# Other cuts for the feed-forward groups and the first output projection in a two-layer diffusion trunk on one core

## The chip, the cores and the metric

One Trainium2 chip, one of its NeuronCores. The metric is the device time of one execution in microseconds. Before the change the median of 3 runs is 2937.39 us (2935.81 to 2938.43).

Five engines work on the core, each through its own instructions in order: TensorE (PE in the profile; PEld is its weight loading), VectorE (DVE), ScalarE (ACT), GpSimd (POOL) and SyncE (SP), which here only issues DMAs.

## The reference, cut to what matters

Input are 512 latent tokens and 128 context tokens, 640 in all, of width 1024. They pass two layers and a last norm. Each layer is: feed-forward, token mixing, feed-forward. Every one of these three parts does

```
h = rmsnorm(x, norm_g) * (1 + m_scale) + m_shift        # m: from the conditioning vector
x = x + [0.5 *] m_gate * part(h)
part of a feed-forward: (silu(h @ w_gate) * (h @ w_up)) @ w2       # inner width 2816
part of a mixing:       concat(y_a, y_b) @ w_out                   # 1024 x 1024
m = silu(cond) @ mod_w[i] + mod_b[i]                               # 9 vectors of 1024 for each layer
```

The mixing of layer 0 is retention beside a gated recurrent block, that of layer 1 a state-space layer beside a delta-rule recurrence. After the norm at the end `y_prompt` and `y_sample` are written, along with four context states.

## The kernel before, in words

**Layout and arithmetic.** Activations lie transposed: `x[d]` is a tile of 128 features by 640 tokens, with 8 such tiles; tokens are worked in two halves of 320 (`h` = 0, 1). Every large product is made three times over from parts (`mm3`, L426): activation and weight are each split into a rounded part and a rest (`whi`/`wlo` for weights, `hs`/`ls` for the normed input, the pairs in `hl` for inner activations), and three matmuls of 128 x 128 by 320 columns sum into one PSUM bank. A weight piece of 128 x 512 is loaded (`load_piece`, L370), rounded by ScalarE (L380) and its rest formed by VectorE (L381), or by GpSimd where `eng=PL` is given (the first two weight tiles of a stage; L400 does the same for the very first). There are 5 buffers for raw pieces and 8 each for `whi` and `wlo`.

**Stages.** Seven, in this order: `f01` (layer 0, feed-forward 1), `m0`, `f02`, `f11`, `m1`, `f12`, `fin`. 

**A feed-forward stage** (`ffn`, L575). The inner width of 2816 is cut into 22 tiles of 128. They are worked in groups, 7, 7, 6 and 2 tiles (`GROUPS`, `GL`, L28). For one group, first the tiles go "up": gate and up product, silu, multiplication, split into a pair of `hl`; 96 matmuls per tile in the plain form. In `f02` from tile 12 on and in `f12` from tile 5 on a form with 7 block products (`up7`) takes their place; it needs sums of the normed input that are made once (`quarters`, L513, started three tiles earlier, in a pool that takes space from the setup of layer 1's state-space part). Then the group goes "down" through `w2`: for each of the four column blocks `dp`, 4 banks of 3 x (tiles of the group) matmuls sum into PSUM banks of the pool `psa` (two banks, tag `acc`), and `add_res` (L545) on VectorE adds each bank, times the gate, to `x`.

**The last group** of a stage goes down in `last_pass` (L551) instead: all of the first half of the tokens, then all of the second. Behind each bank's update the squares for the next norm are summed (`sq`, L452). When the first half is through, its sum over features is taken by a matmul with ones (`stat(0)`, L464), and then `apply(0)` (L476) makes the next stage's normed input for the first half, while the second half of the last pass still goes on; `stat(1)` comes after the last bank, and `apply(1)` after the next stage's first two weight tiles have used the first half. The last group's weights are 4 pieces now, of the 8 buffers.

**Output projections.** `m0` ends in `out_proj` (L749): 8 input tiles, 6 of which go down as above (`w_out0a`, 18 matmuls a bank) and 2 through `last_pass` (`out_last`, L743, with `w_out0b`). At its start `x` is loaded back from DRAM (`load_x`), since the mixing needs its slots. `m1` has its own code for the first 6 (`first_out`) and shares `out_last`.

**Modulation vectors.** Those not needed at once are made by VectorE along the way, in `f01` (9 vectors) and `f11` (7). One vector is 9 steps (`mod_steps`, L329): in each of 8 steps a 512 KB block of `mod_w` is loaded and two 128 x 1024 multiply-adds go into a pair of accumulators (`ma`, L335 and L337, one buffer each), and a ninth step has TensorE reduce them (L342) and finish (L349 to L354). The accumulators come free for the next vector when the L342 matmuls of this one are done. `extra()` (L951) runs 3 steps in `f01` and 2 in `f11`; it is called after each up tile and at the start of each `dp` of a group that goes down (not of the last group), and its first two calls in the program do nothing. What is left is done in one go by `finish_mods()` (L944, called at L679) after the up tiles of the last but one group, ahead of that group's way down.

**Order of the work.** The order on each engine is set beforehand by a planner that runs the program against its own costs: of the instructions that could start, it takes the one that stands first in the program. So an engine may run ahead into later parts when it has nothing else, but what stands earlier in the program goes first as soon as it can start. In `f02` VectorE also prepares the state-space part (`s5_prep`, one call per up tile).

Of the kernel before, what the change touches and what calls it, by code (L numbers as in the profile page):

```python
# [18 lines left out]
P = 128  # L19
D = 1024  # L20
KT = D // P
# [3 lines left out]
HALF = T // 2  # L25
DFF = 2816
NF = DFF // P
GROUPS = [7, 7, 6]  # L28
GL = 2

SEVEN = {(0, 2): 12, (1, 2): 5}
RAWS = 5
# [23 lines left out]
def pack(x):  # L56
    f = np.ascontiguousarray
# [21 lines left out]
    out["w_in0"] = f(w.reshape(KT, P, 12, 256).transpose(2, 1, 0, 3)).reshape(12, P, KT * 256)  # L79
    out["w_v0"] = f(w[:, :, 2].reshape(2, 4, P, 512).transpose(0, 2, 1, 3)).reshape(2, P, 2048)  # L80

    def out_w(n, w, order):
        w = w.reshape(KT, P, 4, 256)[order]
        out[n + "a"] = f(w[:6].transpose(2, 1, 0, 3)).reshape(4, P, 6 * 256)
        out[n + "b"] = f(w[6:].transpose(1, 2, 0, 3)).reshape(P, 2048)
    out_w("w_out0", x["l0_w_out"], [4, 5, 6, 7, 0, 1, 2, 3])
    gates = np.stack([x["l0_lru_wa"], x["l0_lru_wx"]]).reshape(2, 2, 4, 2, 64, 64)
    bd = np.zeros((2, 2, 4, P, P), np.float32)
    bd[..., :64, :64] = gates[:, :, :, 0]
# [4 lines left out]
    out["c1"] = _consts1()  # L94
    w = x["l1_w_in"].reshape(KT, P, 10, 256)
    out["w_in1"] = f(w.transpose(2, 1, 0, 3)).reshape(10, P, KT * 256)
    out_w("w_out1", x["l1_w_out"], list(range(8)))

    def lora_in(a):
        return np.moveaxis(a, 0, 1).reshape(4, P, P) if a.ndim == 3 else a.reshape(4, P, P)  # L100
# [112 lines left out]
def _build(nc, tc, I, O, ctx):  # L213
# [192 lines left out]
    def part(w):  # L406
        return lambda k, o: w(k * 256 + o)
# [141 lines left out]
                                     x[d][:, c0 + a:c0 + b], ALU.mult, ALU.add)  # L549

    def last_pass(w, hl, g, nxt):  # L551
        for h in range(2):
            c = hs_(h)
            for d in range(KT):
                ps = bank(psa, HALF, "acc") if d % 2 else bank(psp, HALF, "gu")
                for i in range(2):
                    mm3(ps, *w(2 * (d // 2) + i, d % 2 * P), hl[i][0][:, c], hl[i][1][:, c], i == 0, i == 1)
                add_res(d, h, ps, g)
                if nxt is not None:
                    nxt.sq(d, h)  # L560
                    if h == 0 and d == 6:
                        ACT.activation(warm, x[d][:, :1], AF.Abs_reciprocal_sqrt, scale=0.0, bias=epsn)
                        DVE.tensor_scalar_mul(zero, warm, 0.0)
                        warmed.append(1)
                    if h == 1 and d == 1:
                        nxt.stat(0)
                        nxt.apply(0)
        if nxt is not None:
            if nxt.final:
                for k in range(4):  # L570
                    nxt.finish(k)
            nxt.stat(1)


    def ffn(l, which, n, gt, mk_next):  # L575
# [52 lines left out]
        for G in GROUPS + [GL]:  # L628
# [52 lines left out]
            if f0 + G == NF:  # L681
                if quarters:
                    close_pool("xt")
                src = I[f"w2_{which}"][l, :, :, f0 * 256:].rearrange("d p n -> p d n")
                ws = [split_piece(load_piece(src[:, d:d + 1, :])) for d in range(4)]
                nxt = nxt()
                last_pass(lambda k, o: [t[:, k % 2 * 256 + o:k % 2 * 256 + o + P] for t in ws[k // 2]], hl, gt(), nxt)
                return nxt
# [52 lines left out]
        return out  # L741

    def out_last(hl, name, g, nxt, w=None):  # L743
        w = w or part(weight(I[name + "b"]))
        nxt = nxt()
        last_pass(w, hl, g, nxt)
        return nxt

    def out_proj(src, name, g, mk_next):  # L749
        nxt = mk_next(load=True)  # L750
        hl = [split_slot(t) for t in src]
        load_x(xs)
        for dp in range(4):
            w = weight(I[name + "a"][dp], 1536)
            for e in range(2):
                for h in range(2):
                    c = hs_(h)
                    ps = bank(psa, HALF, "acc")
                    for i in range(6):
                        mm3(ps, *w(i * 256 + e * P), hl[i][0][:, c], hl[i][1][:, c], i == 0, i == 5)  # L760
                    add_res(2 * dp + e, h, ps, g)
        return out_last(hl[6:], name, g, nxt)

    def log_sigmoid(dst, src, n):
        st = slot()
# [1281 lines left out]
```

## Time and profile before

| what | value |
|---|---|
| median of 3 runs | 2937.39 us |
| the profiled execution | 2936.11 us, its span 2934.3 us |
| PE busy | 2778.1 us, 95% of the span, 25440 matmuls |
| PEld busy | 2627.8 us, 90% |
| DVE busy | 2013.1 us, 69% |
| ACT busy | 1128.8 us, 38% |
| POOL busy | 258.4 us, 9% |
| mean granted TensorE clock | 0.978 of full |

The span is what the profiler saw between the first and the last instruction; 1.8 us of the execution lie outside. A share of busy time is a mean over stages: in most of a feed-forward stage PE is busy without a break, and what it loses lies in a few places, above all where one stage passes to the next. In the rows further down, a bracket behind a row is the idle time of its engine just before it and what ended it; "x" and a number is a count of instructions, merged where they follow each other.

### The profile page before, as it was taken

The page shows a single profiled execution, that of the slowest core. Times are in us where ns is not written, and L with a number is a line of the kernel's source. Part 1 is how long each engine was busy: PE and PEld are TensorE (multiplying, and loading weights), DVE is VectorE, ACT ScalarE, POOL GpSimd, SP SyncE. Part 2 cuts the span into 40 slices and gives each one's busy share as a digit, 9 for nine tenths or more (in the row PEclk, how much of TensorE's full clock was granted, in tenths as well). Part 3 has the DMA queues.
Part 4 walks back from the last instruction along what each step waited for, and adds up shares of the span by engine and source line. Part 5 has one row for each costly group of instructions (what it writes and reads, how often), then busy time and mean ns, then how long its engine had stood idle before and what let it go on. Part 6 is the DMA issues. An engine that isn't in the chain of part 4 may idle for free.

```text
span 2934.3 us, 62170 instructions
## 1 busy us (share of the span) xinstructions
PE 2778.1 (95%) x25440; PEld 2627.8 (90%) x25440; DVE 2013.1 (69%) x4347; ACT 1128.8 (38%) x2337; POOL 258.4 (9%) x226
## 2 busy tenths in 40 slices
PE   6999999999999999998999999998889988999997
PEld 4999999877789998998999999987677877999997
DVE  7686773864798977868665664676766536758676
ACT  4222223584443223435222223334555434424233
POOL 2000000130010000002000001221222103000001
PEclk8999999999999999999999999999999999999999
DMA  8464643211213442234444544352000021123231
GB/s 287 145 198 136 183 142 130 94 44 62 97 60 118 127 116 80 80 97 144 145 142 129 152 139 138 105 156 88 4 4 4 9 87 67 59 79 93 74 91 58
DMA packets 164446, 305.41 MB, mean 104 GB/s; under 512 B 25664, under 2 KB 47808, under 8 KB 164032
## 3 DMA queue, kind: packets, MB, share of 16 engines
q1 hardware_dynamic: 164160, 301.44, 32.8%
q8 instruction: 199, 3.26, 0.5%
q14 instruction: 87, 0.71, 0.1%
HBM read 276.95 MB, written 24.42 MB: 103 GB/s over the span
## 4 chain that ended last, share of the span: by engine, by line
PE 58%; DVE 11%; issue 5%; ACT 2%; POOL 1%; DMA 1%; POOLq 0%; DVEq 0%; ACTq 0%; SPq 0%
PE gu L428 11%; PE gu L429 11%; PE gu L427 11%; PE acc L427 5%; PE acc L428 5%; PE acc L429 5%; PE m L1626 2%; PE acc L1626 1%; PE gu L1626 1%; PE gu L1290 1%; DVE ma L337 1%; DVE s L548 1%; DVE t L496 1%; DVE wlo L381 1%; PE m L429 1%
## 5 line engine op out<-in xcount | busy, mean ns | idle before, releaser
L427 PE MATMUL gu<-s,whi 128*128 128x320 f32 x2804 | 876.1, 313 | 0.8 <-ACT s L1376 0.8
L429 PE MATMUL gu<-s,wlo 128*128 128x320 f32 x2804 | 870.9, 311 | 1.4 <-DVE wlo L381 1.4
L428 PE MATMUL gu<-s,whi 128*128 128x320 f32 x2804 | 871.0, 311 | 0.3 <-DVE s L415 0.3
L380 ACT CAST whi<-raw 128x512 fp32r<-128x512 f32 x624 | 375.9, 610 | 773.0 <-PE acc L428 384.1
L427 PEld LDWEIGHTS gu<-s,whi 128*128 128x128 f32 x2804 | 528.6, 189 | 9.0 <-ACT whi L380 3.5
L429 PEld LDWEIGHTS gu<-s,wlo 128*128 128x128 f32 x2804 | 528.4, 188 | 3.6 <-DVE wlo L381 1.6
L428 PEld LDWEIGHTS gu<-s,whi 128*128 128x128 f32 x2804 | 528.6, 189 | 2.6 <-DVE s L415 0.6
L381 DVE TENSOR_TENSOR wlo<-raw,whi 128x512 fp32r<-128x512 f32 x576 | 381.2, 673 | 152.5 <-ACT whi L380 148.9
L427 PE MATMUL acc<-s,whi 128*128 128x320 f32 x1456 | 452.2, 311 | 6.2 <-DVE s L548 6.2
L429 PE MATMUL acc<-s,wlo 128*128 128x320 f32 x1456 | 451.7, 310 | 0.7 <-DVE wlo L381 0.7
L428 PE MATMUL acc<-s,whi 128*128 128x320 f32 x1456 | 451.6, 310 | 0.0
L427 PEld LDWEIGHTS acc<-s,whi 128*128 128x128 f32 x1456 | 274.1, 188 | 10.6 <-DVE s L548 6.3
L337 DVE SCALAR_TENSOR_TENSOR ma<-mw,cT,ma 128x1024 f32<-128x1024 f32 x224 | 277.0, 1277 | 0.0
L429 PEld LDWEIGHTS acc<-s,wlo 128*128 128x128 f32 x1456 | 274.2, 188 | 1.2 <-DVE wlo L381 0.9
L428 PEld LDWEIGHTS acc<-s,whi 128*128 128x128 f32 x1456 | 274.1, 188 | 0.2 <-issue 0.2
L548 DVE SCALAR_TENSOR_TENSOR s<-acc,hg,s 128x320 f32<-128x320 f32 (+1 forms) x336 | 137.2, 434 | 154.7 <-PE acc L429 152.3
L414 ACT CAST s<-t 128x320 fp32r<-128x320 f32 x212 | 97.0, 458 | 250.7 <-DVE t L641 214.4
L641 DVE TENSOR_TENSOR t<-t,gu 128x320 f32<-128x320 f32 x122 | 59.1, 485 | 167.2 <-PE gu L429 163.5
L400 POOL TENSOR_TENSOR s<-s,s 128x512 fp32r<-128x512 f32 x28 | 40.3, 1464 | 1031.5 <-PE gu L428 891.9
L415 DVE TENSOR_TENSOR s<-t,s 128x320 fp32r<-128x320 f32 x212 | 108.3, 511 | 22.5 <-ACT s L414 22.4
L381 POOL TENSOR_TENSOR wlo<-raw,whi 128x512 fp32r<-128x512 f32 x48 | 67.5, 1425 | 568.8 <-ACT whi L380 555.7
L427 PE MATMUL gu<-s,s 128*128 128x320 f32 x304 | 92.7, 338 | 22.3 <-ACT s L501 20.7
(464 smaller groups left out, 4511.2 us busy)
## 6 DMA issues: line engine op xcount, KB each, us to landing
raw<-w SPq DMA_DIRECT2D x496, 256.0 KB, 2.9
mw<-mod_w SPq DMA_DIRECT2D x144, 512.0 KB, 4.0
raw<-w_in SPq DMA_DIRECT2D x72, 256.0 KB, 3.3
xs<-s SPq DMA_DIRECT2D x16, 320.0 KB, 2.2
s<-xs SPq DMA_DIRECT2D x16, 320.0 KB, 6.0
s<-w SPq DMA_DIRECT2D x16, 256.0 KB, 4.6
raw<-w SPq DMA_DIRECT2D x32, 128.0 KB, 2.2
dca<-ca SPq DMA_DIRECT2D x8, 512.0 KB, 3.8
```

Of the source, the lines that this page charges most:

```text
L337: DVE.scalar_tensor_tensor(acc[s], w, cT[:, k, s:s + 1], acc[s], ALU.mult, ALU.add)
L380: ACT.copy(hi, raw)
L381: (eng or DVE).tensor_sub(lo, raw, hi.bitcast(F32))
L400: PL.tensor_sub(lo[:, :512], raw[:, :512], hi[:, :512].bitcast(F32))
L414: (DVE.tensor_copy if eng is DVE else ACT.copy)(hi, src)
L415: DVE.tensor_sub(lo, src, hi.bitcast(F32))
L427: PE.matmul(ps, whi, xhi, start=start, stop=False, **kw)
L428: PE.matmul(ps, whi, xlo, start=False, stop=False, **kw)
L429: PE.matmul(ps, wlo, xhi, start=False, stop=stop, **kw)
L548: DVE.scalar_tensor_tensor(x[d][:, c0 + a:c0 + b], ps[:, a:b], g[:, d, s:s + 1], x[d][:, c0 + a:c0 + b], ALU.mult, ALU.add)
L641: DVE.tensor_mul(gf, sg, pu)
L1626: PE.matmul(out(rows[h]), lhs(rows[h], h), rhs(rows[h], h), start=i == 0, stop=i == len(terms) - 1, tile_position=(64 * h, 64 * h))
```

## The change

The feed-forward groups become 6, 6, 6 and 4. The output projection of `m0` takes 4 tiles in the first part and 4 in the last pass. `last_pass` takes as many inner tiles as it is given; the last group's weights come as 8 pieces of 512 columns, 256 KB each, in place of 4. `m1` keeps 6 and 2. No matmul is added or dropped.

```diff
-GROUPS = [7, 7, 6]
-GL = 2
+GROUPS = [6, 6, 6]
+GL = 4
...
-    def out_w(n, w, order):
+    def out_w(n, w, order, na):
         w = w.reshape(KT, P, 4, 256)[order]
-        out[n + "a"] = f(w[:6].transpose(2, 1, 0, 3)).reshape(4, P, 6 * 256)
-        out[n + "b"] = f(w[6:].transpose(1, 2, 0, 3)).reshape(P, 2048)
-    out_w("w_out0", x["l0_w_out"], [4, 5, 6, 7, 0, 1, 2, 3])
+        out[n + "a"] = f(w[:na].transpose(2, 1, 0, 3)).reshape(4, P, na * 256)
+        out[n + "b"] = f(w[na:].transpose(1, 2, 0, 3)).reshape(P, (KT - na) * 1024)
+    out_w("w_out0", x["l0_w_out"], [4, 5, 6, 7, 0, 1, 2, 3], 4)
...
     def last_pass(w, hl, g, nxt):
+        n = len(hl)
         for h in range(2):
             c = hs_(h)
             for d in range(KT):
                 ps = bank(psa, HALF, "acc") if d % 2 else bank(psp, HALF, "gu")
-                for i in range(2):
-                    mm3(ps, *w(2 * (d // 2) + i, d % 2 * P), hl[i][0][:, c], hl[i][1][:, c], i == 0, i == 1)
+                for i in range(n):
+                    mm3(ps, *w(n * (d // 2) + i, d % 2 * P), hl[i][0][:, c], hl[i][1][:, c], i == 0, i == n - 1)
...
-                ws = [split_piece(load_piece(src[:, d:d + 1, :])) for d in range(4)]
+                ws = [split_piece(load_piece(src[:, d:d + 1, i:i + 512])) for d in range(4) for i in (0, 512)]
...
-        w = w or part(weight(I[name + "b"]))
+        w = w or part(weight(I[name + "b"], len(hl) * 1024))
...
-            w = weight(I[name + "a"][dp], 1536)
+            w = weight(I[name + "a"][dp], 1024)
...
-                    for i in range(6):
-                        mm3(ps, *w(i * 256 + e * P), hl[i][0][:, c], hl[i][1][:, c], i == 0, i == 5)
+                    for i in range(4):
+                        mm3(ps, *w(i * 256 + e * P), hl[i][0][:, c], hl[i][1][:, c], i == 0, i == 3)
...
-        return out_last(hl[6:], name, g, nxt)
+        return out_last(hl[4:], name, g, nxt)
```

## Rows read from the trace of the kernel before

**Rows 1.** The page: busy us, share of the span, instructions of each engine.

```profile
PE 2778.1 (95%) x25440; PEld 2627.8 (90%) x25440; DVE 2013.1 (69%) x4347; ACT 1128.8 (38%) x2337; POOL 258.4 (9%) x226
```

**Rows 2.** Stretches: start:end, width, busy (count) of PE PEld DVE ACT POOL, clock, DMA, GB/s.

```profile
2510.00:2900.00 390.00, 390.00 (x2661) 390.00 (x2660) 265.84 (x492) 141.54 (x271) 0.00 (x0) 1.00 0.26 78
500.00:570.00 70.00, 65.64 (x427) 63.93 (x426) 51.74 (x113) 37.44 (x81) 16.34 (x14) 0.98 0.23 81
1320.00:1390.00 70.00, 61.72 (x384) 58.94 (x383) 62.04 (x122) 39.07 (x82) 17.82 (x14) 0.95 0.40 137
1815.00:1870.00 55.00, 50.21 (x320) 48.32 (x319) 44.76 (x96) 32.06 (x72) 15.19 (x14) 0.97 0.30 101
836.00:857.00 21.00, 17.44 (x104) 16.53 (x102) 19.65 (x48) 11.15 (x22) 3.88 (x4) 0.92 0.21 62
1100.00:1130.00 30.00, 24.14 (x131) 22.48 (x130) 29.72 (x53) 15.25 (x29) 0.00 (x0) 0.83 0.17 53
531.74:550.23 18.49, 16.70 (x98) 15.93 (x98) 16.88 (x36) 9.20 (x21) 2.72 (x3) 0.91 0.37 129
```

**Rows 3.** What PE waited for in the whole span: us in total, times, longest us.

```profile
PE gu L427 <- ACT s L501: 20.7, 11, 3.6
```

**Rows 4.** Timeline, PE: first matmuls of m0 and f11 on each half, each after its wait.

```profile
533.51 0.56 PE L427 MATMUL gu<-s,s 128*128 128x320 f32 x2 [1.77 <-ACT s L501]
551.65 0.56 PE L427 MATMUL gu<-s,s 128*128 128x320 f32 x2 [1.42 <-ACT s L501]
1369.36 0.56 PE L427 MATMUL gu<-s,s 128*128 128x320 f32 x2 [3.56 <-ACT s L501]
```

**Rows 5.** The stretch from the first matmul of f01's last pass to stat(1).

```profile
517.06:545.20 28.14, 25.83 (x161) 24.80 (x160) 26.53 (x60) 17.06 (x36) 6.54 (x6) 0.94 0.33 123
```

**Rows 6.** Timeline, PE: the two stat matmuls of f01's last pass.

```profile
527.27 0.81 PE L464 MATMUL m<-s,ones 128*128 128x320 f32 x2 [0.52 <-DVE s L459]
545.14 0.70 PE L464 MATMUL m<-s,ones 128*128 128x320 f32 x2
```

**Rows 7.** Timeline: end of f01's last vector but one, and start of the last.

```profile
413.63 1.09 PE L342 MATMUL m<-ma,sel 128*32 128x256 f32 x16
415.30 0.75 DVE L335 TENSOR_SCALAR ma<-mw,cT 128x1024 f32<-128x1024 f32 x1
```

**Rows 8.** Timeline: the same place in f11, to the first updates behind it.

```profile
1731.02 1.09 PE L342 MATMUL m<-ma,sel 128*32 128x256 f32 x16
1732.69 0.75 DVE L335 TENSOR_SCALAR ma<-mw,cT 128x1024 f32<-128x1024 f32 x1
1741.30 0.62 ACT L380 CAST whi<-raw 128x512 fp32r<-128x512 f32 x1 [0.24 <-DMA s<-w_in]
1752.44 1.13 DVE L548 SCALAR_TENSOR_TENSOR s<-acc,hg,s 128x320 f32<-128x320 f32 x3
1753.48 0.69 DVE L381 TENSOR_TENSOR wlo<-raw,whi 128x512 fp32r<-128x512 f32 x1
```

**Rows 9.** Timeline, f02: first and last of DVE's sums for the block form.

```profile
1096.59 0.82 DVE L523 TENSOR_TENSOR xa<-s,s 128x640 f32<-128x640 f32 x1
1123.20 0.82 DVE L415 TENSOR_TENSOR tl<-xb,th 128x640 fp32r<-128x640 f32 x1
```

**Rows 10.** Timeline, PE, the end of the span: the last stat matmul.

```profile
2923.31 1.43 PE L464 MATMUL m<-s,ones 128*128 128x320 f32 x2 [6.77 <-DVE s L459]
```

**Rows 11.** Timeline: m0's first updates, and PE behind them.

```profile
794.32 1.13 DVE L548 SCALAR_TENSOR_TENSOR s<-acc,mod,s 128x320 f32<-128x320 f32 x3 [1.36 <-DMA s<-xs]
794.92 0.41 PE L427 MATMUL acc<-s,whi 128*128 128x320 f32 x1 [1.66 <-DVE s L548]
```

**Rows 12.** Timeline, end of f02: GpSimd's splits and a VectorE split beside them.

```profile
1332.55 4.81 POOL L400 TENSOR_TENSOR s<-s,s 128x512 fp32r<-128x512 f32 x3
1333.11 1.59 DVE L415 TENSOR_TENSOR s<-t,s 128x320 fp32r<-128x320 f32 x1
```

**Rows 13.** The page, costliest groups: a VectorE split of 128 x 320, usual length.

```profile
L415 DVE TENSOR_TENSOR s<-t,s 128x320 fp32r<-128x320 f32 x212 | 108.3, 511 | 22.5 <-ACT s L414 22.4
```

More of the change, by code (lines that the diff above doesn't have):

```diff
@@ L96, in pack @@
     out["w_in1"] = f(w.transpose(2, 1, 0, 3)).reshape(10, P, KT * 256)
-    out_w("w_out1", x["l1_w_out"], list(range(8)))
+    out_w("w_out1", x["l1_w_out"], list(range(8)), 6)
     def lora_in(a):
```

## The prediction

> **What bounds the kernel now.** I read the busy times first, then the table of stretches, then what TensorE (PE) waited for, then the timeline at the places that these name. PE is busy for 95% of the span [rows 1], and the change adds and drops no matmul, so only PE's lost time can move. In the middle of a feed-forward nothing is lost: 390 us of f12 hold 2661 matmuls of 320 columns, 0.1466 us each [rows 2]. With this pitch every stretch can be priced: its width less its count times 0.1466 (a record missing from the trace would make a loss look larger, but the 390 us show that few are missing). f01 to m0 (500 to 570): 70 - 427 x 0.1466 = 7.4 us lost. f02 to f11 (1320 to 1390): 70 - 56.3 = 13.7. f11 to m1 (1815 to 1870): 55 - 46.9 = 8.1. m0's last pass (836 to 857): 21 - 15.2 = 5.8. The first block-form tile of f02 (1100 to 1130): 30 - 19.2 = 10.8 [rows 2].
>
> The starts of stages lose it in two waits for the next norm, one for each half of the tokens, L501 being the biggest entry of PE's waits with 20.7 us in 11 [rows 3]: in m0 1.77 and 1.42 us, in f11 the second is 3.56 us [rows 4]. Around them the clock drops: from 531.74 to 550.23 the granted mean is 0.91, which is 0.18 of 18.49 us, 3.3 us, at the lower level of 1.2 GHz, after PE had stood, and it costs half of that, 1.7 us [rows 2]. What ends last there is VectorE (DVE): from the last pass's first matmul to `stat(1)` it is busy 26.5 of 28.1 us [rows 5]. The last pass itself has 96 matmuls, 14.1 us. It is too short for the updates, squares and norm beside it.
>
> **Part 1, what goes: waits at the ends of feed-forwards.** With four tiles the last pass has 192 matmuls, 28.1 us, and the same 26.5 us of DVE work beside it. `stat(0)` ran 10.2 us after the pass began, 3.2 us behind the end of its first half at 7.0 [rows 5, 6]. Now the first half ends at 14.1, DVE has kept up, and `stat(0)` comes at some 16. From it to the first normed tile took 6.2 us (527.27 to 533.51) [rows 4, 6]: ready at 22, and the pass goes on to 28.1. So the first wait goes, with its slow clock. From `stat(0)` to `stat(1)` DVE had 17.9 us of work [rows 6]: 16 + 17.9 = 34, which is 6 us after the pass. From `stat(1)` to the first tile of the second half took 6.5 us (545.14 to 551.65) [rows 4, 6]: ready 12.5 us after the pass. PE has two weight tiles of the first half to do meanwhile, 96 x 0.1466 = 14.1 us. The margin is 1.6 us, and the tiles behind the first come slowly, so I leave a part of the loss: 3 us of 7.4 at f01, 3.5 of 8.1 at f11, and 5 of 13.7 at f02, where modulation steps of f11 mix into the same chain. Gain 4.4 + 4.6 + 8.7 = 17.7. Bounds: 0, if DVE is as late as now, and 29.2, if all goes. At the end of the span PE stood for 6.77 us before the last `stat` [rows 10], while DVE worked off its backlog; what the last bank itself needs (two updates, a square, an addition) is some 2.5 us, at half a microsecond for an operation of this size [rows 13]. Gain 4 (0 to 4.3).
>
> **Part 2, m0.** Its last pass gains in the same way: of 5.8 us I leave 1, gain 4.8. Against it, its first banks now have 12 matmuls in place of 18. The first update waited for `x` to come back from DRAM until 794.3, and PE, with two banks to fill, stood 1.66 us [rows 11]. Two banks now fill in 3.5 us in place of 5.3: 1.8 more. Together a gain of 3 (-4 to 6; the lower end is a slow clock of 1.7 and another such wait on top).
>
> **Part 3, f02's block form.** Four tiles' worth of sums occupied DVE from 1096.59 to 1124.0, just while PE went from tile 11 to tile 12, the first that uses them [rows 9]. In groups of six, tile 11 ends a group, and 6 x 48 x 0.1466 = 42.2 us of way down lie between 11 and 12. The sums are ready long before tile 12. Of the 10.8 us I leave 2, since the sums stand ahead of the group's updates in the program and may hold a few of them: gain 8.8 (2 to 10.8). The preparations at one per up tile come 4 and 4 around a way down in place of 5 and 3: 0 (-3 to 3).
>
> **Part 4, what the change adds: `finish_mods` comes two tiles earlier.** f01 has 9 vectors of 9 steps, 81. Calls of `extra` ahead of `finish_mods`: 20 tiles + 8 blocks - 2 = 26 now, 78 steps, and 24 after, 72. f11 has 63; 28 x 2 = 56 now, 52 after. What decides is not the number but where a vector can start. A vector's accumulators come free when PE has reduced the one before, and PE, which always has a backlog, reaches those matmuls where the program has them. Now step 72 of f01 is behind tile 17 and step 54 of f11 behind tile 18: the last vector starts 1.67 us behind its predecessor's reduction [rows 7, 8], while PE has two and one more tiles to do. In f01 that hides it. In f11 it does not quite: 16 multiply-adds keep DVE from 1732.69 to 1752.44, and a weight split that could start at 1741.9 stands behind them until 1753.48, and so do the group's first updates, the first of three at 1752.44 [rows 8].
>
> After the change both last steps of the vector before (72 and 54) lie directly ahead of the third group's way down, behind tile 17. Call the end of that tile T. The vector starts at T + 1.67 and takes the 19.8 us of f11 less the 2.1 of other work that lay between, plus 1.0 for tile 17's own product and split: all done at T + 20.4. PE does the reduction (1.1) and its finish (0.4), and two banks of 18 matmuls (5.3) until T + 6.8; the third bank needs an update that DVE takes only after the vector. Behind it on DVE stand four updates per column block and its next weight pieces, and for those PE waits. So PE stands 13.6 us, and then runs at the lower clock for a while, 1.7 as above: 15.3 us, in f01 and in f11, 30.6 together. Bounds: 0, if the planner lets the updates in between, and 40, if a lower clock or late weight pieces last longer. Row 1741.30 against 1753.48 is near the full price. In f01, 6 multiply-adds a column block fall on 10.6 us of PE work in place of 12.3; DVE's lead covers most, 1 us (0 to 5).
>
> The other edits cost nothing that ends a path: 8 half pieces become 4 whole ones in each feed-forward, loaded ahead of use while PE has its backlog; without that cover each would show as a wait for `raw`, of which there is none in PE's waits. The 8 pieces fill all 8 buffers, the last four coming free in the last up tile's second half, before the pass.
>
> **The sum.** Gains 17.7 + 4 + 3 + 8.8 = 33.5, costs 30.6 + 1 = 31.6: 1.9 us less. The profiled execution took 2936.11 (a span of 2934.3 and 1.8 outside), 1.3 below the median of 2937.39. Forecast 2934.
>
> **Rivals.** *The starts become seamless.* If DVE's holes are filled as well as now, both waits go, and the 11.5 us left in part 1 go too: 2934 - 11.5 = 2922.5. For it: the margin of 1.6 us is positive without any credit. Against: f11's start is held by steps that stay.
>
> *GpSimd holds VectorE in the pass (slower).* Now the next stage's second weight tile is split on GpSimd before or early in the last pass. With all 8 buffers taken, its four pieces can start only as the pass's pieces come free, in its second half, beside the norm's chain. Beside GpSimd's splits a VectorE split took 1.59 us in place of the usual 0.51 [rows 12, 13], 1.1 more. Four pieces a start, four starts: 4 x 4 x 1.1 = 17.6, 2934 + 17.6 = 2951.6. From half of it on (8.8) the kernel is slower by more than can be told from no change. Against: the first half has 6 us to spare, and some of the holds fall on idle time. On the Trainium skill: "SBUF — State Buffer", section "SBUF: two separate sides", says that VectorE and GpSimd share one port pair as an exclusive lock for a whole instruction, with no sharing of bandwidth, where a VectorE instruction has two SBUF inputs. By it an estimate is one full GpSimd split per hold, and the sum would go above 2951.6; row 1333.11 agrees in kind, and shows less than a full split.
>
> *The sums of part 3 hold the group before tile 12.* They start 8.5 us ahead of its end now; 27 us of them would run 18 us into the way down, against 5.3 us that two banks cover: up to 8 us come back, 2942.
>
> *The vectors do not hold PE.* If updates pass between the multiply-adds, part 4 is gone: 2934 - 30.6 = 2903. Against: rows 8.
>
> **Chances and range.** A difference below 0.2% (5.9 us) can't be told from none. Forecast 0.42 with its own range of 2926 to 2942; seamless starts 0.24; GpSimd 0.17; sums 0.09; no hold 0.08. Faster: 0.24 + 0.08 and 0.09 of the forecast's, 0.41. Slower: 0.14 of GpSimd's, 0.04 of the sums', 0.02, together 0.20. The rest, 0.39, within. 2914 to 2952 leaves out the case of no hold and the far ends.
>
> **What would show it.** Right: PE stands some 13 us at the start of the third group's way down in f01 (near 400) and f11 (near 1700), with L337 as what ends it; no L501 wait on a first half at f02's end and f01's; less than 3 us before the last `stat`; 1100 to 1130 without a gap. Wrong: no such stand, or waits on L501 as large as now, or new ones for `x` in m0 above 6 us.

## The result, and the profile after

The changed kernel takes 2951.26 us (median of 6 runs, 2945.78 to 2952.95) against 2935.74 of the kernel before beside it: ratio 1.0051, 95% interval 1.0038 to 1.0064. It is slower by 15 us, where 2 us less were forecast. The profiled execution has a span of 2948.8 us, 14.5 more than before.

The page of the kernel after: busy us, share and instructions of each engine (before: [rows 1]).

```profile
PE 2770.6 (94%) x25440; PEld 2623.6 (89%) x25440; DVE 2023.3 (69%) x4331; ACT 1127.8 (38%) x2321; POOL 261.1 (9%) x226
```

The work is the same; what differs is where PE stands. Stretches of the kernel after, columns as in [rows 2]: the ends of f01, f02 and f11 (from 16 us before `stat(0)` to 25 us after `stat(1)`), the first block-form tile of f02, and the two places where `finish_mods` now falls.

```profile
517.34:581.78 64.44, 60.89 (x395) 60.33 (x394) 51.32 (x106) 32.14 (x70) 11.21 (x10) 0.95 0.24 82
...
1325.52:1390.00 64.48, 57.03 (x355) 54.69 (x354) 62.56 (x110) 32.79 (x70) 16.33 (x12) 0.95 0.45 150
1824.88:1889.21 64.33, 60.77 (x395) 60.22 (x394) 51.19 (x103) 32.14 (x70) 11.21 (x10) 0.95 0.31 102
...
1100.00:1135.00 35.00, 33.61 (x228) 33.06 (x227) 26.59 (x52) 11.82 (x20) 0.00 (x0) 1.00 0.21 62
...
395.00:440.00 45.00, 32.90 (x225) 29.59 (x224) 31.62 (x47) 10.71 (x20) 0.00 (x0) 0.85 0.42 137
1700.00:1750.00 50.00, 37.90 (x260) 34.61 (x259) 32.28 (x47) 8.21 (x15) 0.00 (x0) 0.86 0.48 159
```

Width less count times 0.1466 gives the loss, as before the change. The three ends lose 6.5, 12.4 and 6.4 us, where they lost 7.4, 13.7 and 8.1 [rows 2]: hardly anything is gained. The block form's 10.8 us [rows 2] are 1.6. The last two rows lose 12.0 and 11.9 at a clock of 0.85 and 0.86; the kernel before has 317 and 351 matmuls in these stretches.

The timeline of the kernel after, PE: the matmuls behind its largest waits.

```profile
418.48 1.78 PE L342 MATMUL m<-ma,sel 128*32 128x256 f32 x6 [12.02 <-DVE ma L337]
...
546.97 0.61 PE L427 MATMUL acc<-s,whi 128*128 128x320 f32 x1 [3.55 <-DVE s L548]
...
807.65 0.64 PE L427 MATMUL acc<-s,whi 128*128 128x320 f32 x1 [4.52 <-DVE s L548]
...
869.75 0.38 PE L427 MATMUL acc<-s,whi 128*128 128x320 f32 x1 [3.58 <-DVE s L548]
...
1341.52 1.44 PE L464 MATMUL m<-s,ones 128*128 128x320 f32 x2 [2.48 <-DVE s L459]
...
1373.84 0.41 PE L427 MATMUL gu<-s,s 128*128 128x320 f32 x1 [2.99 <-ACT s L501]
...
1726.23 2.20 PE L342 MATMUL m<-ma,sel 128*32 128x256 f32 x10 [12.03 <-DVE ma L337]
...
1854.51 0.61 PE L427 MATMUL acc<-s,whi 128*128 128x320 f32 x1 [3.56 <-DVE s L548]
...
2937.83 1.44 PE L464 MATMUL m<-s,ones 128*128 128x320 f32 x2 [5.26 <-DVE s L459]
```

The two waits of 12.0 were forecast. The waits of 3.55, 3.58 and 3.56 on `acc` were not: PE stands inside the last pass, for the last bank of the second half. The wait for the norm's first half (the first of [rows 4]) is gone at f01's end, and so is its like at f11's; at f02's end the second half is waited for 2.99 us (3.56 in [rows 4]).

**Ledger.** How much later the same event comes than before: `m0`'s first L942 matmul 11.6 us (694.4 to 706.0); just ahead of f02's block form 15.1 and behind it 5.9 (at equal counts of matmuls, rows below); f11's first silu 4.5 (1362.5 to 1367.0); `m1`'s first matmul of L1239 in the line numbers of before 16.6 (1906.3 to 1923.0); the last `stat` 14.5.

PE alone, from the span's start to the same count of matmuls: before and after, ahead of the block form, then behind it (start:end, width, busy and count, clock, DMA, GB/s).

```profile
0.00:1095.00 1095.00, 1037.28 (x6904) 0.98 0.41 130
0.00:1110.10 1110.10, 1036.19 (x6904) 0.98 0.41 129
...
0.00:1135.00 1135.00, 1071.43 (x7101) 0.98 0.40 127
0.00:1140.90 1140.90, 1065.60 (x7101) 0.98 0.40 127
```

| stretch | forecast, us | measured, us |
|---|---|---|
| f01 to L942 (vectors 15.3, f01 1, start -4.4) | +11.9 | +11.6 |
| m0 and f02 to the block form | -3 | +3.5 |
| block form | -8.8 | -9.2 |
| end of f02, start of f11 | -8.7 | -1.4 |
| f11 to L1239 (vectors 15.3, start -4.6) | +10.7 | +12.1 |
| m1 to the last `stat` | -4 | -2.1 |
| sum | -1.9 | +14.5 |

Inside the first and the fifth line two misses cancel: by counts of matmuls the vectors cost 13.6 and 13.8 us in place of 15.3 each, and the starts gained some 2 us each in place of 4.4 and 4.6. The largest misses are m0 with f02 up to the block form (6.5 us) and the end of f02 (7.3).

What happens in f01's last pass after the change: timeline of DVE, ACT and POOL, and one row of f02's.

```profile
532.51 0.62 ACT L380 CAST whi<-raw 128x512 fp32r<-128x512 f32 x1 [1.23 <-PE acc L428]
533.20 1.29 POOL L381 TENSOR_TENSOR wlo<-raw,whi 128x512 fp32r<-128x512 f32 x1 [16.23 <-ACT whi L380]
537.27 2.81 POOL L381 TENSOR_TENSOR wlo<-raw,whi 128x512 fp32r<-128x512 f32 x2 [1.52 <-DVE t L473]
537.41 1.50 DVE L474 SCALAR_TENSOR_TENSOR s<-t,t 128x320 f32<-128x320 f32 x1
538.95 1.47 DVE L496 SCALAR_TENSOR_TENSOR t<-s,ns,s 128x320 f32<-128x320 f32 x1
545.70 0.41 DVE L548 SCALAR_TENSOR_TENSOR s<-acc,hg,s 128x192 f32<-128x192 f32 x1
...
807.04 1.13 DVE L548 SCALAR_TENSOR_TENSOR s<-acc,mod,s 128x320 f32<-128x320 f32 x3 [2.47 <-DMA s<-xs]
...
1341.64 2.23 DVE L337 SCALAR_TENSOR_TENSOR ma<-mw,cT,ma 128x1024 f32<-128x1024 f32 x1
```

The rounding of the next stage's second weight tile (L380) waits for a matmul of the pass to release a `whi` buffer. So GpSimd's L381 falls at 533 to 540, in the pass's second half; before, it stood at 512 to 522, ahead of the pass and in its first 5 us. The kernel before, POOL, the first and the last two of the four splits:

```profile
512.25 1.30 POOL L381 TENSOR_TENSOR wlo<-raw,whi 128x512 fp32r<-128x512 f32 x1
...
518.51 3.12 POOL L381 TENSOR_TENSOR wlo<-raw,whi 128x512 fp32r<-128x512 f32 x2
```

Beside the splits VectorE's norm operations take 1.50 and 1.47 us in the kernel after, in place of 0.49 and 0.54 elsewhere. The fourth bank's update (545.70), whose buffer the last bank needs, stands behind the whole `apply(0)` in the program, and VectorE came to it when most of that was done.

### The profile page after: what moved, and what is told of

Read it like the earlier page. It is cut to its first block, busy times and chain, and to the rows that moved or that the text cites. A ratio compares the mean times of both kernels' runs of the same rounds, so it can differ in the third digit from the quotient of the medians.

```text
span 2948.8 us, 62032 instructions
## 1 busy us (share of the span) xinstructions
PE 2770.6 (94%) x25440; PEld 2623.6 (89%) x25440; DVE 2023.3 (69%) x4331; ACT 1127.8 (38%) x2321; POOL 261.1 (9%) x226
## 4 chain that ended last, share of the span: by engine, by line
PE 73%; DVE 15%; issue 5%; ACT 3%; DMA 2%; POOL 2%; SPq 0%; POOLq 0%; DVEq 0%; ACTq 0%
PE gu L429 15%; PE gu L428 15%; PE gu L427 15%; PE acc L427 6%; PE acc L429 6%; PE acc L428 6%; PE m L1627 2%; PE acc L1627 1%; PE gu L1627 1%; DVE ma L337 1%; DVE s L548 1%; DVE t L496 1%; DMA mw<-mod_w 1%; DVE s L415 1%; DVE wlo L381 1%
## 5 line engine op out<-in xcount | busy, mean ns | idle before, releaser
L427 PE MATMUL gu<-s,whi 128*128 128x320 f32 x2884 | 899.2, 312 | 0.8 <-ACT s L1377 0.8
L429 PE MATMUL gu<-s,wlo 128*128 128x320 f32 x2884 | 894.4, 310 | 0.0
L428 PE MATMUL gu<-s,whi 128*128 128x320 f32 x2884 | 893.5, 310 | 0.0
L380 ACT CAST whi<-raw 128x512 fp32r<-128x512 f32 x608 | 375.0, 620 | 711.2 <-PE acc L428 380.8
L427 PEld LDWEIGHTS gu<-s,whi 128*128 128x128 f32 x2884 | 542.2, 188 | 8.0 <-ACT whi L380 3.1
L428 PEld LDWEIGHTS gu<-s,whi 128*128 128x128 f32 x2884 | 542.3, 188 | 2.0 <-issue 0.2
L429 PEld LDWEIGHTS gu<-s,wlo 128*128 128x128 f32 x2884 | 542.2, 188 | 1.9 <-issue 0.8
L381 DVE TENSOR_TENSOR wlo<-raw,whi 128x512 fp32r<-128x512 f32 x560 | 385.4, 695 | 160.0 <-ACT whi L380 154.5
L427 PE MATMUL acc<-s,whi 128*128 128x320 f32 x1376 | 430.4, 313 | 22.0 <-DVE s L548 20.1
L428 PE MATMUL acc<-s,whi 128*128 128x320 f32 x1376 | 428.8, 312 | 0.0
L429 PE MATMUL acc<-s,wlo 128*128 128x320 f32 x1376 | 428.3, 311 | 0.0
L427 PEld LDWEIGHTS acc<-s,whi 128*128 128x128 f32 x1376 | 260.9, 190 | 29.2 <-issue 16.2
L337 DVE SCALAR_TENSOR_TENSOR ma<-mw,cT,ma 128x1024 f32<-128x1024 f32 x224 | 278.4, 1282 | 0.0
L428 PEld LDWEIGHTS acc<-s,whi 128*128 128x128 f32 x1376 | 261.0, 190 | 0.2 <-issue 0.2
L429 PEld LDWEIGHTS acc<-s,wlo 128*128 128x128 f32 x1376 | 260.9, 190 | 0.0
L641 ACT ACTIVATE t<-gu 128x320 f32<-128x320 f32 x122 | 52.8, 435 | 146.2 <-PE gu L429 146.1
L427 PE MATMUL gu<-s,s 128*128 128x320 f32 x304 | 96.0, 328 | 12.3 <-ACT s L501 10.7
```

Of the source, the lines that this page charges most:

```text
L337: DVE.scalar_tensor_tensor(acc[s], w, cT[:, k, s:s + 1], acc[s], ALU.mult, ALU.add)
L380: ACT.copy(hi, raw)
L381: (eng or DVE).tensor_sub(lo, raw, hi.bitcast(F32))
L427: PE.matmul(ps, whi, xhi, start=start, stop=False, **kw)
L428: PE.matmul(ps, whi, xlo, start=False, stop=False, **kw)
L429: PE.matmul(ps, wlo, xhi, start=False, stop=stop, **kw)
```

## The experiments

Each is timed against the kernel before on the same chip; ratios carry their 95% interval. The changed kernel has 1.0051 (1.0038 to 1.0064).

**mods_late: the vectors.**

```diff
             if f0 + G + GL == NF:
-                finish_mods()
                 nxt = mk_next(load=True)
...
+                finish_mods()
                 nxt = nxt()
                 last_pass(...)
```

> The changed kernel with finish_mods moved from before the third group's way down to before the last group's way down; nothing else. Theory A (the early call of finish_mods costs what the profile shows): both stands of 12.0 us behind an L342 reduction (406 and 1714) go, with the low clock behind them; the stretches around them cost 13 and 13.9 us more than before, so about 26 us less than the changed kernel, 2925 us, 10 us below the kernel before. Rival B (the vectors' work has to be done somewhere, and PE waits for it elsewhere): the stand returns beside the last group's tiles, before the last pass or before the next stage's first tile, 8 to 15 us each, and the time stays within 8 us of the changed kernel's 2951.

Measured: 2921.95 us, ratio 0.9952 (0.9940 to 0.9964). Both stands are gone; in f01 a wait of 1.63 us is left. Stretches of mods_late:

```profile
395.00:440.00 45.00, 43.37 (x312) 41.55 (x311) 35.90 (x57) 12.17 (x23) 0.00 (x0) 1.00 0.44 153
1675.00:1725.00 50.00, 50.00 (x351) 49.18 (x350) 35.80 (x54) 11.73 (x22) 0.00 (x0) 1.00 0.38 125
```

Theory A holds, 29 us less (26 expected), with the 3.55 us inside the passes as before. The steps find room beside the third group's way down.

**apply_d3 and bank7: the wait inside the pass.** apply_d3:

```diff
-                    if h == 1 and d == 1:
+                    if h == 1 and d == 3:
                         nxt.stat(0)
                         nxt.apply(0)
```

> The changed kernel with stat(0) and apply(0) put behind the fourth bank of the last pass's second half in place of the second. Theory A (PE stands 3.55 us inside the pass because the updates of the fourth bank on stand behind apply(0) in the program, and the last bank wants the fourth's buffer): the waits of 3.55, 3.59 and 3.56 us on acc in f01, m0 and f11 go, and no wait for the first half of the next normed input of over 1 us takes their place: 9 to 14 us less than the changed kernel, 2938 to 2942. Rival B (VectorE has too much work in the second half whatever its order): the wait moves to the next stage's first matmuls on L501, 2 to 4 us a start, and the time is within 4 us of the changed kernel.

Measured: 2947.07 us, ratio 1.0040 (1.0028 to 1.0052), which can't be told from the changed kernel's. Its profiled execution was the fastest of its six, with a span 8.1 us shorter than the changed kernel's. The three waits on `acc` are gone; PE waits longer for the norm's first half at f02's end and m1's (1.95 us there after the change). Timeline of apply_d3, PE:

```profile
1347.58 0.90 PE L427 MATMUL gu<-s,s 128*128 128x320 f32 x2 [4.79 <-ACT s L501]
...
2483.14 0.90 PE L427 MATMUL gu<-s,s 128*128 128x320 f32 x2 [3.61 <-ACT s L501]
```

bank7:

```diff
-                ps = bank(psa, HALF, "acc") if d % 2 else bank(psp, HALF, "gu")
+                ps = bank(psm, HALF, "m") if (h, d) == (1, 7) else bank(psa, HALF, "acc") if d % 2 else ...
```

> The changed kernel in which the last bank of the last pass's second half comes from the pool of two banks that the statistics use, so it doesn't wait for the fourth bank's update. Theory A (PE stands for a buffer while it has other work): the 3.55 us in f01, m0 and f11 go and PE runs on into the next stage's first tile; the gain of 3.55 us and some slow clock each, 10 to 13 us, stays if the second half of the norm is ready in time. Rival B (VectorE is late, and the buffer is only where it shows first): the time comes back as a wait for the second half on L501 in each start, and the kernel is within 4 us of the changed one.

Measured: 2946.18 us, ratio 1.0040 (1.0026 to 1.0054). The waits on `acc` are gone, and PE stands for the second half's sum instead. Timeline of bank7, PE, f01's `stat(1)` (m0 and f11 have 3.72 and 3.09):

```profile
552.96 0.81 PE L464 MATMUL m<-s,ones 128*128 128x320 f32 x2 [3.09 <-DVE s L459]
```

Both medians come out nearer to rival B: 4 and 5 us less, where theory A asked for some 10. In the profile of apply_d3 f01, m0 and f11 gain 3 to 4 us each and under 3 come back at f02's and m1's ends, so a new order moves the wait only in part; why the median keeps no more of it is not shown. The reading that the buffer is where it shows first, and that PE waits for a late VectorE, rests on the next experiments, which make VectorE earlier.

**no_pool_split and before_no_pool: GpSimd.** The same edit in both kernels; the rests of a stage's first two weight tiles are left out, and so are those of m1's pieces, which GpSimd forms too. ScalarE writes a scaled copy in their place. In `split_piece`, and alike in `weight_in_slots`:

```diff
-        (eng or DVE).tensor_sub(lo, raw, hi.bitcast(F32))
+        (ACT.mul(lo, raw, 2.0 ** -12) if eng is PL else DVE.tensor_sub(lo, raw, hi.bitcast(F32)))
```

> The changed kernel in which GpSimd forms no rests of the first two weight tiles of a stage: ScalarE writes a scaled copy into their place instead, so the rests of these tiles are not computed (left out); VectorE's work is the same. Theory C (GpSimd's splits hold VectorE's operations in the second half of the pass, and this makes the wait on acc): VectorE's operations that took 1.2 to 1.5 us there (four in f01, 3.3 us over their usual length) fall to 0.5, and the waits of 3.55 us shrink to under 1 us: 8 to 14 us less. Theory A (the order of the program makes the wait, the holds only lengthen it): the waits keep over half their length or are replaced by waits on L501, 0 to 8 us less.

> The kernel before, with the same edit as no_pool_split: the rests of the first two weight tiles of a stage are not formed (left out). In the changed kernel this took 30.8 us away, of which the profile puts 2.6 at the very beginning, some 6.5 inside m1, and 4 to 7 at each of the four starts of stages that the change touches. Theory C (the change moved GpSimd's splits of the second weight tile into the second half of the last pass, where they hold VectorE beside the norm; in the kernel before they lie ahead of the pass and cost little): only the beginning and m1 are gained, 7 to 12 us, so 2923 to 2928. Rival D (GpSimd's splits cost the starts as much in the kernel before): 25 to 32 us less, 2903 to 2910.

Measured: 2920.48 us, ratio 0.9950 (0.9938 to 0.9962), and for the kernel before 2915.44 us, 0.9934 (0.9921 to 0.9946). The changed kernel gains 31 us, over twice what theory C asked; by the profiles 5 to 9 at each of the four starts, 2.6 at the very beginning and some 6 in m1, and the 3.55 us in f01 are 1.00. The end of f01, of no_pool_split and then of before_no_pool:

```profile
514.99:574.63 59.64, 58.64 (x397) 58.09 (x396) 48.42 (x106) 33.53 (x74) 5.83 (x6) 1.00 0.26 89
```

```profile
508.72:566.40 57.68, 53.48 (x355) 51.84 (x354) 47.54 (x107) 37.93 (x84) 5.72 (x6) 1.00 0.23 83
```

Losses of 1.4 and 5.6 us, against 6.5 and some 7.4 with GpSimd's splits: f01's end gains 5.1 after the change and 1.8 before it. Without these splits the change costs 5.0 us (2920.5 - 2915.4) and not 15.5, so some 10.5 us of its cost hang on them, those of the first tiles and of m1 included. Both expectations for the kernel before missed: it gained 20 us, of which some 8 lie in m0's output projection (from its first matmul to `stat(0)` 62.0 us, 787.8 to 849.9, and 54.3 with the edit, 784.6 to 838.9), where the splits of f02's first two tiles stand (799.9 to 838.5); neither theory had priced that.

**dve_split.**

```diff
-                    ws = [n.w0, part13(weight(src[1], eng=PL))]
+                    ws = [n.w0, part13(weight(src[1]))]
```

and alike in the two other places of a second tile.

> The changed kernel with the rests of each stage's second weight tile formed by VectorE (0.68 us each, four a start) in place of GpSimd (1.3 us each and more). Theory C (GpSimd's instructions hold VectorE's beside them): 2.7 us of work on VectorE take the place of holds of 3.3 us in f01, and they can be put behind the norm's own work, so the starts gain a part of what no_pool_split gained at them, 6 to 15 us less than the changed kernel, 2936 to 2945. Rival (VectorE is what ends last at the starts, so more work on it makes them later): 4 to 10 us more than the changed kernel.

Measured: 2930.46 us, ratio 0.9984 (0.9975 to 0.9992): 21 us less, more than theory C asked. End of f01 in dve_split, 1.9 us lost:

```profile
514.47:573.98 59.51, 59.06 (x393) 57.59 (x392) 49.94 (x110) 31.98 (x70) 5.58 (x6) 1.00 0.25 88
```

So the same splits cost this kernel less on VectorE than beside it on GpSimd.

**plain8 and plain12: why the splits moved.** Both without the block form (`SEVEN = {}`), to make room; plain12 has `PIECES = 12`.

> The changed kernel without the block form: all up tiles of f02 and f12 are plain ones (96 matmuls each in place of 84), so PE has more matmuls, and the time is not to be compared with the other kernels: 27 tiles, 12 matmuls of 0.147 us more each, 47 us, 2996 to 3002. It is the other half of plain12. The waits of 3.55 us inside the last passes of f01, m0 and f11 are there, since nothing before f02's twelfth tile differs.

> plain8 with 12 buffers for split weight pieces in place of 8, nothing else. Theory C with buffers (the splits of the next stage's second weight tile stand in the second half of the pass because the pass's eight pieces hold every buffer until then): GpSimd's L381 stands ahead of the pass or in its first half, as in the kernel before, the waits of 3.55 us on acc in f01, m0 and f11 go or fall under 1.5 us, and the time is 8 to 18 us below plain8. Rival (raw buffers, the DMA or the order of the program keep them there): the splits and the waits stay, within 4 us of plain8.

Measured: 2993.62 us, ratio 1.0196 (1.0179 to 1.0213), and 2971.80 us, 1.0122 (1.0107 to 1.0137): four buffers are worth 21.8 us, a little over the expected range; plain8 itself came 2 us under its own. 17 of the 21.8 are there at `m1`'s first matmul of L1239 in the line numbers of before (1933.1 and 1915.8), the others come later. The second tile's splits at f01's end in plain8, then in plain12 (POOL), and the ends of f01, f02, f11, plain8 first:

```profile
532.50 2.55 POOL L381 TENSOR_TENSOR wlo<-raw,whi 128x512 fp32r<-128x512 f32 x2 [16.25 <-ACT whi L380]
```

```profile
512.08 1.30 POOL L381 TENSOR_TENSOR wlo<-raw,whi 128x512 fp32r<-128x512 f32 x1
...
518.38 2.81 POOL L381 TENSOR_TENSOR wlo<-raw,whi 128x512 fp32r<-128x512 f32 x2
```

```profile
516.63:578.53 61.90, 58.35 (x395) 57.80 (x394) 51.23 (x106) 32.05 (x70) 11.21 (x10) 1.00 0.25 85
...
1336.70:1400.13 63.43, 58.43 (x387) 56.25 (x386) 50.54 (x101) 32.69 (x69) 11.25 (x10) 0.97 0.18 60
1836.02:1899.39 63.37, 59.82 (x395) 59.26 (x394) 51.22 (x103) 32.15 (x70) 11.20 (x10) 0.97 0.31 104
```

```profile
517.61:577.14 59.53, 59.07 (x393) 57.60 (x392) 50.71 (x109) 31.94 (x70) 9.15 (x9) 1.00 0.27 94
...
1331.98:1391.51 59.53, 57.84 (x393) 55.63 (x392) 51.30 (x105) 32.21 (x69) 8.98 (x9) 1.00 0.21 72
1825.45:1884.97 59.52, 58.90 (x392) 57.34 (x391) 50.20 (x102) 32.01 (x70) 12.80 (x12) 1.00 0.34 111
```

4.0, 6.7 and 5.5 us lost with 8 buffers, 1.9, 1.9 and 2.1 with 12. The splits are ahead of the pass and in its first 5 us again, and inside the last passes of f01, m0, f02 and f11 no wait of over 0.6 us on `acc` is left. This settles why the splits moved: the pass's eight pieces hold the buffers.

**hold_mods and late_dve_hold: f02's end.** f11's multiply-adds read a copy of the conditioning vector that depends on the norm's second half, so that none can start in f02's last pass.

```diff
                     if f == 0 and h == 0:
                         n.apply(1)
+                        if (l, which) == (1, 1):   # mod_steps reads this copy in place of cT
+                            DVE.scalar_tensor_tensor(cT1, n.r[:, HALF:HALF + 256], 0.0, cT, ALU.mult, ALU.add)
```

> The changed kernel in which the multiply-adds of f11's modulation vectors cannot start before the second half of f11's first norm (they read a copy of the conditioning vector that is made from it). Theory E (in f02's last pass VectorE fills its spare time with twelve of these steps of 1.3 to 2.2 us, and so reaches the updates and stat(0) late): the wait of 2.49 us before stat(0) goes, and of the 2.99 us on the second half a part: 4 to 8 us less than the changed kernel. They have to be done later: if VectorE lacks the time then, 0 to 3 us of it come back at f11's end. Rival: the wait before stat(0) comes from the updates themselves and from GpSimd, and stays; the time is within 2 us of the changed kernel, or more by a later end of f11's vectors.

Measured: 2949.87 us, ratio 1.0051 (1.0039 to 1.0064): nothing. The wait before `stat(0)` is gone, as theory E said, and the one inside the pass stands in its place. Timeline of hold_mods, PE:

```profile
1352.37 0.61 PE L429 MATMUL acc<-s,whi 128*128 128x320 f32 x1 [3.55 <-DVE s L550]
...
1374.39 0.56 PE L429 MATMUL gu<-s,s 128*128 128x320 f32 x2 [3.30 <-ACT s L503]
```

The other half of the same place is dve_split, which takes GpSimd's splits out and leaves the multiply-adds in: PE still waits there. Timeline of dve_split, PE:

```profile
1327.05 0.81 PE L464 MATMUL m<-s,ones 128*128 128x320 f32 x2 [2.49 <-DVE s L459]
...
1358.29 0.56 PE L427 MATMUL gu<-s,s 128*128 128x320 f32 x2 [3.50 <-ACT s L501]
```

**The repairs together.** late_dve is mods_late and dve_split in one; late_dve_m62 has m0 in 6 and 2 besides; before_dve_late is the kernel before with both repairs; all_dve is late_dve_m62 with every other rest on VectorE too (`PL.tensor_sub` in `weight_in_slots`, `eng=PL` in m1); late_dve_hold adds the edit of hold_mods to late_dve; all_dve_hold is that with the other rests on VectorE. m0_62 is the changed kernel with 6 and 2 in m0.

Expected of m0_62:

> The changed kernel with m0's output projection in 6 and 2 tiles again; the feed-forwards keep 6, 6, 6 and 4. If m0's 4 and 4 costs what the two profiles show (4.2 us more at the waits for x, 2 us less around its last pass), this is 1 to 4 us less than the changed kernel, about 2949. Rival (the shorter last pass costs its 5.8 us again, and the x waits are the same): 2 to 5 us more.

Expected of late_dve:

> The changed kernel with both repairs: finish_mods ahead of the last group's way down, and the rests of each stage's second weight tile formed by VectorE. Alone they took 29.3 and 20.8 us off the changed kernel's 2951.3. If the two faults are independent: 2901, within 4. Rival: they share VectorE's time (with the bursts gone, its steps reach into the starts), and 6 us or more of the sum come back, 2907 and above.

Expected of late_dve_m62:

> late_dve with m0's output projection in 6 and 2 tiles again. m0_62 took 3.0 us off the changed kernel, where GpSimd's holds stood in m0's last pass. Theory (the 4 and 4 costs the wait for x, 4 us more than 6 and 2, which stays in every version): 2 to 5 us below late_dve. Rival (without the holds the longer last pass gives back its 4.8 us, and only the holds hid that): 0 to 4 us above late_dve.

Expected of before_dve_late:

> The kernel before with the same two repairs, so that late_dve less this is what the new groups and the new cut of m0 are worth by themselves. Theory F (the gains of the forecast are there once its two faults are out: 17.7 at the starts, 8.8 at the block form, 2 to 4 at the end of the span, less 4 in m0): this kernel is 24 to 33 us above late_dve, 2925 to 2934. Rival G (the repairs help the kernel before as much, and the groups are worth only the block form's 9 us and little more): 2908 to 2916.

Expected of late_dve_hold:

> late_dve (2905.2) with f11's first multiply-adds held back until the second half of its first norm, as in hold_mods. Theory (at f02's end two things fill VectorE, the splits of the second weight tile and the early steps of f11's vectors, and either alone keeps the start late): with both out, the stretch around f02's last pass loses 2 to 4 us in place of 11, and the kernel is 5 to 9 us below late_dve, 2896 to 2900. Rival (hold_mods took nothing away, since the steps have to be done anyway and come back later in f11): within 2 us of late_dve.

Expected of all_dve:

> late_dve_m62 with every rest of a weight piece formed by VectorE, those of a stage's first weight tile and of m1's pieces too (in no_pool_split these were left out on GpSimd with a gain of 5 us inside m1). Theory C (a hold costs VectorE more than the 0.68 us of doing the split itself): 2 to 8 us below late_dve_m62. Rival (ahead of the starts and in m1 VectorE has no time to spare and GpSimd's holds fall on idle time): 0 to 6 us above.

Expected of all_dve_hold:

> All repairs on the changed kernel, with its 4 and 4 in m0: finish_mods late, every rest of a weight piece on VectorE, f11's steps held back. all_dve, with 6 and 2 in m0 and the steps not held, has 2888.1. If the holding back is worth here what the start of f11 still loses there (6.1 us, of which 2 to 3 stay): 2883 to 2886. Rival (6 and 2 is better in m0 without GpSimd, or the holding back costs as much later): 2887 to 2893.

| kernel | median, us | ratio to before |
|---|---|---|
| m0_62 | 2948.25 | 1.0040 (1.0028 to 1.0052) |
| before_dve_late | 2923.91 | 0.9964 (0.9952 to 0.9977) |
| late_dve | 2905.20 | 0.9899 (0.9885 to 0.9912) |
| late_dve_m62 | 2905.88 | 0.9898 (0.9883 to 0.9913) |
| late_dve_hold | 2899.52 | 0.9875 (0.9859 to 0.9892) |
| all_dve_hold | 2891.08 | 0.9849 (0.9833 to 0.9864) |
| all_dve | 2888.14 | 0.9841 (0.9828 to 0.9854) |

With both faults out, the new groups and m0's new cut are worth 18.7 us (2923.9 - 2905.2), between what F and G said; the profiled spans differ by 26.1, and by counts of matmuls f01's end gains 6.0 there, f11's 5.5 and f02's 3.0 (forecast 4.4, 4.6 and 8.7). m0's cut is worth nothing either way that these runs can tell. The two repairs give 46 us together, 4 less than their sum. Holding back f11's steps, worth nothing alone, takes about 6 us off late_dve, just at the edge of the noise (the two intervals touch): f02's end loses 10.4 us in late_dve and 5.9 in late_dve_hold, more than the 2 to 4 expected, next two rows.

```profile
1298.05:1359.05 61.00, 53.84 (x345) 52.09 (x345) 60.49 (x112) 31.91 (x69) 9.57 (x8) 0.97 0.42 147
```

```profile
1298.47:1358.00 59.53, 55.24 (x366) 53.50 (x365) 54.72 (x108) 33.33 (x72) 11.44 (x10) 1.00 0.38 130
```

So that end had two causes, each enough to keep VectorE late. all_dve beats both kernels, by 1.6% and 2.1%; it and all_dve_hold can't be told apart, and the 2883 to 2886 expected of the latter were not reached. Page of all_dve; GpSimd has 150.7 us left, and PE reaches 96%:

```profile
PE 2755.7 (96%) x25440; PEld 2610.3 (90%) x25440; DVE 2018.7 (70%) x4407; ACT 1128.5 (39%) x2321; POOL 150.7 (5%) x150
```

## Why the prediction was wrong

**The step that failed** is the last of part 4: "The other edits cost nothing that ends a path", with the eight pieces that "fill all 8 buffers". The prediction saw that the buffers would be full and asked only whether the pass's own pieces are there in time. They are. What it left out of the sum is the next stage's second tile, which wants the same buffers: its splits waited for the pass to free them, fell on GpSimd beside the norm, and VectorE was held by up to 1 us at a time. So of the 17.7 us that part 1 put down as gain at the starts 4 to 5 came, and of the 4.8 in m0's last pass hardly anything. The omitted tile stood among the rivals, as *GpSimd holds VectorE in the pass*, with 0.17, the right place and the right mechanism (plain12, no_pool_split, dve_split) and a price of 17.6 us; some 10.5 were measured on the pair without these splits. That its total of 2951.6 falls on the measured time is luck: the misses below make up the difference. With the same two repairs in both kernels the new groups give 18.7 us, where the other parts of the sum come to 32.5, so this step is not the whole miss.

**Part 1, starts** (gain 17.7 forecast). "DVE has kept up" holds for the first half at f01: VectorE had the sum ready 16.1 us after the pass began, as forecast (16), and PE took `stat(0)` at 17.6, behind two banks of the second half. The first-half waits went at all three ends. (The row of [rows 5] starts at the pass's second bank, so `stat(0)` before ran 11.1 us after the pass began and not 10.2.) The second half failed: VectorE, held by GpSimd, got to the fourth bank's update so late that PE stood 3.55 us, and the clock fell (0.95 over the stretch). In f01 `stat(1)` came 41.1 us after the pass began, where 34 were forecast; with 12 buffers (plain12) it is 36.1. Timeline of the kernel after, then of plain12, PE, f01's `stat(1)`; the passes begin at 515.73 and 516.01:

```profile
556.78 0.70 PE L464 MATMUL m<-s,ones 128*128 128x320 f32 x2
```

```profile
552.14 0.81 PE L464 MATMUL m<-s,ones 128*128 128x320 f32 x2 [0.23 <-DVE s L459]
```

So with the buffers there, the arithmetic of part 1 is borne out: what it left as loss was 3, 5 and 3.5 us, and plain12 loses 1.9, 1.9 and 2.1. f02's end has a cause besides that the prediction named only as something mixing in: VectorE fills the pauses of this pass with f11's multiply-adds, 1.27 us each and up to 2.23 beside GpSimd. The kernel before has one of them in its shorter pass. plain12, without the block form, has none in a pass of the same length, so its 1.9 us at f02 owe something to that too; why they start so early here is not shown.

**The end of the span:** 5.26 us stand before the last `stat`, 1.5 less than in [rows 10] and not 4. The last bank's own chain was priced at 2.5; the backlog ahead of it, beside GpSimd's final products (L482), was taken to vanish. That cause is argued from the timeline, not tried.

**Part 2, m0:** against the 11.6 us by which the stage is late, PE came 1.7 us earlier to the wait for `x`, as forecast (1.8), but `x` itself came 1.1 later, and 4.52 us were the wait (1.66 in [rows 11]); two more, of 1.01 and 1.74, follow (one of 1.86 before), and the last pass had its 3.58. By counts of matmuls m0 lost 4.4 us where 3 were to be gained, and f02 up to the block form gave back 0.9. Why `x` is later was not tried.

**Part 3, block form:** right, 9.2 gained (8.8).

**Part 4, the vectors:** right in place and cause. PE did two banks and then stood 12.0 us and not 13.6, with L337 as what ended it, as forecast; with the slow clock 13.6 in f01 and 13.8 in f11 (15.3 each), and mods_late puts both together at 29 (30.6).

**On the Trainium skill:** of GpSimd's two splits from 537.27 to 540.08 the first takes 1.30 us and the second begins at 538.52; the two VectorE operations beside them end 0.34 us after the end of the first split and 0.34 after that of the second, somewhat less than their usual lengths. "SBUF — State Buffer", section "SBUF: two separate sides", says that GpSimd and a VectorE operation with two SBUF inputs share one pair of ports, and that whichever starts first keeps it for its whole instruction. By that rule a hold lasts until the split ends, and the trace agrees: what the prediction read as "less than a full split" is a VectorE operation that came in the middle of one: the split beside row 1333.11 of [rows 12] runs from 1332.55 to 1334.36, and the operation ends 0.34 us later.

## What to carry to other kernels

When a step takes more buffers of a rotating pool, look for who takes the next ones, on which engine that work runs and beside what it will now fall; a load that was early for free can land on the path. A wait that comes back in another place when a bank or the order of instructions is changed points at the engine that is late: take work off that engine, or off the other engine that holds it. Of two causes that each keep an engine late, removing one shows nothing (hold_mods), so an experiment without effect is repeated once the other is out.

## What the runs showed of the hardware

- A rest of 128 x 512 costs GpSimd 1.3 us and VectorE 0.68, and beside it a VectorE operation took some 1 us more than usual (1.50 in place of 0.49, 1.59 in place of 0.51). All the rests on VectorE were faster: all_dve is 18 us below late_dve_m62, more than the 2 to 8 expected.
- In the profiled executions the same stand of 3.55 us in f01's pass goes with a granted mean of 0.95 of full over the stretch after the change and of 1.00 in plain8; the stretches lose 6.5 and 4.0 us. So the slow clock behind a stand of this size is not certain, and cost some 2.5 us where it came.
